# Gated DeltaNet layer on one core: the diagonal blocks of the chunk inverse reach V and T64 by VectorE block transposes with a strided output instead of through DRAM

## The chip, the cores and the metric

The kernel runs on one core of a Trainium2 chip. A core has five engines with instruction streams of their own: TensorE (PE; its weight loads are listed as PEld), VectorE (DVE), ScalarE (ACT), GpSimd (POOL) and SyncE (SP), which here only issues DMAs. Each engine works through its stream in order. The metric is the device time of one launch in microseconds (us).

## What is computed

The program has one layer (`DEPTH = 1`): RMSNorm, a gated DeltaNet mixer with its residual add, and a final RMSNorm, on 2048 tokens of width 1024, 8 heads of 128. The part that matters here is the chunked delta rule. In the reference a chunk has 64 tokens and the triangular matrix of each chunk and head is inverted by a solve:

```
a_mat = einsum("nbhid,nbhjd->nbhij", kb, k) * decay_strict
t_mat = triangular_solve(eye + a_mat, eye, left_side=True, lower=True, unit_diagonal=True)
u = t_mat @ (v * beta);   w = t_mat @ (kb * exp(g))
# then over the chunks of a head, one after the other:
v_new = u_c - w_c @ state
o_c   = qd_c @ state + attn_c @ v_new
state = state * gend_c + kend_c^T @ v_new
```

The kernel computes the same outputs with chunks of 128 tokens, so each inverse is 128 x 128.

## The kernel before, in words

**Tiling.** The sequence is cut into two super-blocks of 1024 tokens (`sb` 0 and 1). For each, `phase0` normalises and transposes x into `xh` and `xl` (a split of float32 into two parts that TensorE takes at full rate). Then come 16 units, one for each head and super-block: `project` (K, Q, V, Z; 24 matmuls of 128x512 for each of the eight outputs of a unit, and a short convolution behind K, Q and V), `decay` and `k_side` (the matrix U of each of the 8 chunks of the unit), `invert` (V, the inverse of 8 chunks), `v_side`, and `recur`, the serial loop over the 8 chunks: k S, then rho (DVE), then V rho, then n (ACT), then the update of S (DVE). `recur(u)` needs the V of its own unit; there are two V buffers, used in turn. At the end 16 output tiles (`out_tile`) are multiplied with w_out, 8 for each super-block; those of super-block 0 can run while the last units do.

**The inverse.** `invert` takes the four 32x32 diagonal blocks of each of the 8 chunks. They go through DRAM (`d1`) into the tile A, each block on four partitions; then 16 pairs of DVE instructions (TENSOR_TENSOR into a temporary, TENSOR_REDUCE into X) solve all blocks at once. Partition (i, c, g) of X holds rows 4m+g of block i of chunk c. The result has to go to two places: `T64` (blocks with the row on the partition, one buffer for all units) and the diagonal blocks of `V` (transposed). Then four groups of small matmuls build the off-diagonal parts: p1 (16 of 32x32, from T64), p2 (24 of 32x32, from V and Y), p3 (8 of 64x64, from T64), p4 (8 of 64x64, from V). ACT copies between them (Y, V), and one DVE copy writes the block of T64 that p3 needs.

**What sets the order.** All instructions are first recorded in a `Plan` with priorities, estimated durations and dependencies. `Plan.schedule` runs a list scheduler over them and `issue` emits them in the order found. So an edit in `invert` can move instructions everywhere. All instructions are emitted at one line, L354 of the profile; they are told apart by the tiles' names. In the profile `half` is the pool of 512-wide tiles (Y is one of them), `big` that of 1024-wide ones (A and U among them), `bank` a PSUM bank, `rnd` a split weight, `T` is T64, `d` is `d1` or `d2`. A float32 matmul shows as two records.

Of the kernel before, what the change touches and what calls it, by code (L numbers as in the profile page):

```python
# [29 lines left out]
C = SB // P  # L30
# [328 lines left out]
def tile_gated_deltanet(ctx: ExitStack, tc: tile.TileContext, x, a_norm_w, w_in, conv_w,  # L359
                        a_log, dt_bias, o_norm_w, w_out, final_w, consts, out):  # L360
    x, out, w_in, w_out = x[0], out[0], w_in[0], w_out[0]
# [12 lines left out]
    nc = Plan(tc, cp, pp, bufs, shared)  # L374
# [3 lines left out]
    def dram(tag, shape, bufs):  # L378
        n = turn.get(tag, 0)
        turn[tag] = n + 1  # L380
        if n < bufs:
            turn[tag, n] = dp.tile(shape, F32, name=f"{tag}{n}")
        return turn[tag, n % bufs]

    def st(shape, dtype, tag):
        return nc.tile(tag, shape, dtype)

    def ps(tag, shape=(P, TB)):
        a = nc.tile(tag, (P, TB), F32, psum=True)[0:shape[0], 0:int(np.prod(shape[1:]))]
        return a.rearrange("p (c k) -> p c k", k=shape[2]) if len(shape) > 2 else a  # L390
# [55 lines left out]
    T64 = cp.tile([P, C, 64], F32, name="T64")  # L446
# [196 lines left out]
    def chunked(a):  # L643
        return a.rearrange("p (c k) -> p c k", k=P)

    def bc(col, n=P):
        return col.unsqueeze(2).broadcast_to([P, col.shape[1], n])
# [73 lines left out]
    R = [slice(32 * i, 32 * i + 32) for i in range(4)]  # L721

    def invert(un):
        U, V = chunked(un["U"]), Vs[un["i"] % 2]

        d1 = dram("d1", [4, C, 32, 32], 2)
        for i in range(4):
            nc.sync.dma_start(d1[i].rearrange("c r k -> r c k"), U[R[i], :, R[i]])
        A = st([P, 32, 32], F32, "A")
        nc.sync.dma_start(A, d1.rearrange("i c r k -> (i c) (r k)").unsqueeze(1).broadcast_to([4 * C, 4, 1024]))  # L730

        nc.vector.memset(A.rearrange("p a b -> p (a b)")[:, ::33], 0.0)
        pair = st([P, 15, 32], F32, "pair")
        up = A.rearrange("p a b -> p (a b)")[:, 34:34 + 66 * 15:66]
        nc.vector.tensor_tensor(out=pair, in0=A[:, 2::2, :], in1=bc(up, 32), op=ALU.mult)
        nc.vector.tensor_tensor(out=A[:, 1:30:2, :], in0=A[:, 1:30:2, :], in1=pair, op=ALU.add)
        nc.vector.memset(A.rearrange("p a b -> p (a b)")[:, ::33], 1.0)
        X = st([P, 8, 32], F32, "X")
        nc.scalar.copy(X, rows4)
        for c in [*range(29, 0, -2), 0]:  # L740
            n, m0, w = 32 - c, c // 4, 2 if c else 1
            tmp = st([P, 8, 2, 32], F32, "pair")[:, m0:, 0:w, 0:n]
            nc.vector.tensor_tensor(out=tmp, in0=X[:, m0:, c:].unsqueeze(2).broadcast_to([P, 8 - m0, w, n]),
                                    in1=A[:, c:c + w, c:].unsqueeze(1).broadcast_to([P, 8 - m0, w, n]), op=ALU.mult)
            nc.vector.tensor_reduce(out=X[:, m0:, c:c + w], in_=tmp, axis=AX.X, op=ALU.add)
        d2 = dram("d2", [32, 4, C, 32], 2)
        for g in range(4):
            nc.sync.dma_start(d2[g::4].rearrange("m i c k -> (i c) m k"), X[g::4])
        for i in range(4):
            b = (i % 2) * 32  # L750
            nc.sync.dma_start(T64[R[i], :, b:b + 32], d2[:, i])
        for i in range(4):
            b = (i % 2) * 32
            nc.vector.transpose(out=V[R[i], :, R[i]], in_=T64[R[i], :, b:b + 32])
        p1 = ps("inv", (P, C, 32))
        nc.after = T64[R[2], :, 0:32],
        for c in range(C):
            nc.tensor.matmul(p1[R[1], c], lhsT=U[R[0], c, R[1]], rhs=T64[R[0], c, 0:32], start=True, stop=True)
            nc.tensor.matmul(p1[R[3], c], lhsT=U[R[2], c, R[3]], rhs=T64[R[2], c, 0:32], start=True, stop=True)
        Y = st([P, C, 64], F32, "Y")[:, :, 0:32]  # L760
        nc.scalar.copy(Y[R[1]], p1[R[1]])
        nc.scalar.copy(Y[R[3]], p1[R[3]])
        p2 = ps("inv", (P, C, 32))
        nc.after = Y[R[3]], V[R[3], :, R[3]]
        for c in range(C):
            nc.tensor.matmul(p2[R[0], c], lhsT=Y[R[1], c], rhs=V[R[1], c, R[1]], start=True, stop=True)
            nc.tensor.matmul(p2[R[2], c], lhsT=Y[R[3], c], rhs=V[R[3], c, R[3]], start=True, stop=True)
            nc.tensor.matmul(p2[R[1], c], lhsT=V[R[1], c, R[1]], rhs=Y[R[1], c], start=True, stop=True)
        nc.scalar.copy(V[R[0], :, R[1]], p2[R[0]])
        nc.scalar.copy(V[R[2], :, R[3]], p2[R[2]])  # L770
        nc.vector.tensor_copy(T64[R[1], :, 0:32], p2[R[1]])
        p3 = ps("inv", (P, C, 64))
        for c in range(C):
            nc.tensor.matmul(p3[64:128, c], lhsT=U[0:64, c, 64:128], rhs=T64[0:64, c], start=True, stop=True)
        Y2 = st([P, C, 64], F32, "Y")
        nc.scalar.copy(Y2[64:128], p3[64:128])
        p4 = ps("inv", (P, C, 64))
        for c in range(C):
            nc.tensor.matmul(p4[0:64, c], lhsT=Y2[64:128, c], rhs=V[64:128, c, 64:128], start=True, stop=True)
        nc.scalar.copy(V[0:64, :, 64:128], p4[0:64])  # L780
# [135 lines left out]
    for u in range(NU):  # L916
        un = dict(i=u, sb=u // H, h=u % H, xh=xhs, xl=xls, g=gt, w=w_first if u == 0 else {})
        last = u % H == H - 1
        nc.prio = float(u)
        if prev is not None:  # L920
            recur(prev)
        if u == 0:
            nc.prio = -0.72
        project(un, ((KI, 0), (QI, 0)), 2 if u == 0 else 1)
        nc.prio = float(u)
        decay(un)
        k_side(un, 0)
        project(un, ((KI, 1), (QI, 1)))
        k_side(un, 1)
        nc.prio = u - 0.5  # L930
        invert(un)
        nc.prio = float(u)
        project(un, ((VI, 0), (ZI, 0), (VI, 1), (ZI, 1)) if last else ((VI, 0), (VI, 1), (ZI, 0), (ZI, 1)))
        v_side(un)
        if last and u < NU - 1:
            nc.prio = u - 0.5
            xhs, xls, pba = phase0(u // H + 1)
            gt = gates(pba)
        prev = un
# [3 lines left out]
    for sb in range(NSB):  # L943
        for t in range(SB // P):
            i = sb * C + t
# [42 lines left out]
```

## Time and profile before

| | |
|---|---|
| median of 3 runs | 1285.72 us (1285.3 to 4319.13) |
| profiled execution, device time | 1284.4 us |
| its span, first to last instruction | 1282.6 us |
| mean granted clock of TensorE | 0.986 |
| busy: PE, PEld, DVE, ACT, POOL | 1245.6, 1041.1, 933.9, 615.1, 159.6 us |
| DMA: packets, of them under 512 B | 162439, 58817 |
| DMA: MB, share of 16 engines (q1) | 123.00, 32.7% |

Busy time is the time in which an engine has an instruction in work. The time outside the span is what the launch needs before its first and after its last instruction. TensorE has two clock levels, 1.2 and 2.4 GHz; a granted clock of 1.00 is the upper one, 0.50 the lower.

### The profile page before, as it was taken

The page shows a single profiled execution, that of the slowest core. Times are in us where ns is not written, and L with a number is a line of the kernel's source. Part 1 is how long each engine was busy: PE and PEld are TensorE (multiplying, and loading weights), DVE is VectorE, ACT ScalarE, POOL GpSimd, SP SyncE. Part 2 cuts the span into 40 slices and gives each one's busy share as a digit, 9 for nine tenths or more (in the row PEclk, how much of TensorE's full clock was granted, in tenths as well). Part 3 has the DMA queues.
Part 4 walks back from the last instruction along what each step waited for, and adds up shares of the span by engine and source line. Part 5 has one row for each costly group of instructions (what it writes and reads, how often), then busy time and mean ns, then how long its engine had stood idle before and what let it go on. Part 6 is the DMA issues. An engine that isn't in the chain of part 4 may idle for free.

```text
span 1282.6 us, 21318 instructions
## 1 busy us (share of the span) xinstructions
PE 1245.6 (97%) x8093; PEld 1041.1 (81%) x8093; DVE 933.9 (73%) x2181; ACT 615.1 (48%) x1301; POOL 159.6 (12%) x277
## 2 busy tenths in 40 slices
PE   6999799999999999989999999999999999999997
PEld 5788688888888888878887888888888888887886
DVE  5678677858776868786787787778777788854643
ACT  6664265544465436656543645453645464231221
POOL 4211011101011101120010101010101010101000
PEclk9999799999999999999998999999999999999999
DMA  7140432220433042422223323204222435545731
GB/s 221 34 113 22 103 82 76 67 78 18 120 81 124 14 122 77 119 51 85 79 52 90 86 63 74 72 14 120 76 83 52 167 94 172 183 156 173 255 106 66
DMA packets 162439, 123.00 MB, mean 96 GB/s; under 512 B 58817, under 2 KB 141346, under 8 KB 162338
## 3 DMA queue, kind: packets, MB, share of 16 engines
q1 hardware_dynamic: 162338, 121.66, 32.7%
q8 instruction: 63, 1.03, 0.3%
q14 instruction: 38, 0.31, 0.1%
HBM read 100.46 MB, written 21.17 MB: 95 GB/s over the span
## 4 chain that ended last, share of the span: by engine, by line
PE 93%; DVE 4%; ACT 1%; DMA 1%; issue 0%; SPq 0%; POOLq 0%; DVEq 0%; ACTq 0%
PE bank L354 93%; DVE half L354 2%; DVE X L354 1%; DVE big L354 1%; DMA big<-in_a_norm_w_dram 0%; DVE rnd L354 0%; DVE xl L354 0%; ACT half L354 0%; ACT rnd L354 0%; ACT xh L354 0%; SPq L354 0%; DMA d<-X 0%; DVE V L354 0%; ACT V L354 0%; ACT n L354 0%
## 5 line engine op out<-in xcount | busy, mean ns | idle before, releaser
L354 PE MATMUL bank<-xh,rnd 128*128 128x512 f32 (+1 forms) x2624 | 878.2, 404 | 6.1 <-ACT rnd L354 4.7
L354 PEld LDWEIGHTS bank<-xh,rnd 128*128 128x128 f32 x2624 | 484.8, 190 | 96.6 <-ACT rnd L354 5.3
L354 PE MATMUL bank<-xl,rnd 128*128 128x512 f32 (+1 forms) x1328 | 534.4, 403 | 0.8 <-DVE xl L354 0.8
L354 PEld LDWEIGHTS bank<-xl,rnd 128*128 128x128 f32 x1328 | 252.6, 190 | 46.0 <-DVE xl L354 1.6
L354 DVE SCALAR_TENSOR_TENSOR half<-raw,vcol,half 128x512 f32<-128x512 f32 x288 | 214.2, 746 | 64.5 <-ACT half L354 61.7
L354 ACT ACTIVATE half<-half 128x512 f32<-128x512 f32 x128 | 81.1, 633 | 94.2 <-DVE half L354 93.1
L354 ACT ACTIVATE n<-bank,nb 128x128 f32<-128x128 f32 x128 | 46.8, 366 | 145.1 <-PE bank L354 144.9
L354 ACT CAST rnd<-big 128x1024 fp32r<-128x1024 f32 x80 | 83.2, 1046 | 65.7 <-PE bank L354 46.0
L354 ACT COPY raw<-bank 128x512 f32<-128x512 f32 x96 | 56.4, 587 | 106.4 <-PE bank L354 105.9
L354 DVE TENSOR_TENSOR rnd<-big,rnd 128x1024 fp32r<-128x1024 f32 x80 | 97.4, 1218 | 12.9 <-ACT rnd L354 12.5
L354 DVE TENSOR_TENSOR half<-X,big 128x6 f32<-128x6 f32 (+15 forms) x256 | 94.8, 370 | 5.4 <-ACT X L354 1.4
L354 DVE TENSOR_REDUCE X<-half 128x2 f32<-128x6 f32 (+15 forms) x256 | 91.9, 359 | 4.1
L354 DVE SCALAR_TENSOR_TENSOR S<-S,dend,bank 128x128 f32<-128x128 f32 x128 | 44.0, 344 | 69.7 <-PE bank L354 69.0
L354 ACT ACTIVATE half<-big 128x512 bf16<-128x512 f32 (+1 forms) x48 | 37.1, 773 | 102.5 <-DVE big L354 56.7
L354 POOL COPY halo<-raw 128x3 f32<-128x3 f32 x72 | 21.7, 301 | 476.9 <-ACT raw L354 437.1
L354 ACT ACTIVATE half<-raw,vcol 128x512 f32<-128x512 f32 x96 | 69.3, 722 | 6.6 <-DVE vcol L354 1.5
L354 DVE SCALAR_TENSOR_TENSOR rho<-bank,eg,half 128x128 f32<-128x128 f32 x128 | 44.2, 345 | 31.2 <-PE bank L354 30.7
L354 PEld LDWEIGHTS bank<-n,half 128*128 128x128 f32 x256 | 47.2, 191 | 12.9 <-ACT n L354 3.3
L354 PEld LDWEIGHTS bank<-rho,V 128*128 128x128 f32 x256 | 47.5, 193 | 11.8 <-ACT V L354 1.7
L354 PEld LDWEIGHTS bank<-S,half 128*128 128x128 f32 x256 | 47.2, 193 | 11.7 <-DVE S L354 2.5
L354 POOL TENSOR_TENSOR sk<-ssk,phalf 128x4 f32<-128x4 f32 x32 | 35.4, 1107 | 157.3 <-DVE ssk L354 154.0
L354 ACT ACT_TABLE_LOAD x42 | 53.9, 1283 | 1.5 <-PEq L972 0.7
(113 smaller groups left out, 1558.1 us busy)
## 6 DMA issues: line engine op xcount, KB each, us to landing
big<-in_a_w_in_dram SPq DMA_DIRECT2D x64, 512.0 KB
big<-in_x_dram SPq DMA_DIRECT2D x32, 512.0 KB
big<-gd SPq DMA_DIRECT2D x16, 512.0 KB
half<-gd SPq DMA_DIRECT2D x32, 256.0 KB
big<-d SPq DMA_DIRECT2D x16, 512.0 KB
yd<-half SPq DMA_DIRECT2D x32, 256.0 KB
big<-yd SPq DMA_DIRECT2D x16, 512.0 KB
big<-rd SPq DMA_DIRECT2D x16, 512.0 KB
```

Of the source, the lines that this page charges most:

```text
L354: ins = getattr(getattr(self.tc.nc, op[6]), op[7])(*args, **kwargs)
```

## The change

The tile `d2` in DRAM goes, with its four DMAs from X and its four DMAs into T64 for each unit (128 in all). In their place DVE transposes X straight into the diagonal blocks of V: for block i the instruction reads 32 partitions (c, g) by 8 x 32 elements (m, k), transposes each 32x32 square, and writes partition k, so that element (m, c, g) lands at `V[k, c, 4m+g]`. The output is strided: runs of four float32, and after each run a jump to the next chunk. Then T64 is filled from V by three plain transposes (blocks 0, 2 and 1; the fourth block of T64 was read by nothing but the old transposes). Four DVE transposes from T64 to V go, seven come.

```diff
-        d2 = dram("d2", [32, 4, C, 32], 2)
-        for g in range(4):
-            nc.sync.dma_start(d2[g::4].rearrange("m i c k -> (i c) m k"), X[g::4])
         for i in range(4):
+            nc.vector.transpose(out=V[R[i], :, R[i]].rearrange("p c (m g) -> p m c g", g=4), in_=X[R[i]])
+        for i in (0, 2, 1):
             b = (i % 2) * 32
-            nc.sync.dma_start(T64[R[i], :, b:b + 32], d2[:, i])
-        for i in range(4):
-            b = (i % 2) * 32
-            nc.vector.transpose(out=V[R[i], :, R[i]], in_=T64[R[i], :, b:b + 32])
+            nc.vector.transpose(out=T64[R[i], :, b:b + 32], in_=V[R[i], :, R[i]])
```

The scheduler makes a new order of it on every engine. Up to the end of unit 0's X loop the order of PE and DVE is the old one; three later places are shown.

DVE, end of unit 0's X loop, before (X is reduced for the last time in the first row; `big_103` is A of unit 1; `half_454` a convolution):

```order
L354 TENSOR_REDUCE X_158<-half_647 128x8
L354 SCALAR_TENSOR_TENSOR half_454<-raw_115,vcol,half_454 128x512
L354 MEMSET big_103 128x32
L354 TENSOR_TENSOR half_482<-big_103 128x480
...
L354 STREAM_TRANSPOSE V_85<-T_84 32x8x32
L354 TENSOR_TENSOR half_647<-X_158,big_103 128x8x15
L354 TENSOR_REDUCE X_158<-half_647 128x4x2
L354 STREAM_TRANSPOSE V_85<-T_84 32x8x32
L354 TENSOR_TENSOR half_482<-X_158,big_103 128x10x17
```

and the same place now:

```order
L354 TENSOR_REDUCE X_156<-half_645 128x8
L354 SCALAR_TENSOR_TENSOR half_452<-raw_113,vcol,half_452 128x512
L354 STREAM_TRANSPOSE V_85<-X_156 32x8x8x4 x4
L354 STREAM_TRANSPOSE T_84<-V_85 32x8x32 x3
L354 MEMSET big_101 128x32
L354 TENSOR_TENSOR half_480<-big_101 128x480
```

The four old transposes stood between pairs of unit 1's X loop; the seven new ones stand in one piece ahead of that loop. In the other units they stand in one piece too.

PE, the inverse of unit 0 and the start of `recur(0)`, before (`bank_172<-xh,rnd` is the last of 24 projection matmuls into that bank):

```order
L354 MATMUL bank_172<-xh_337,rnd_491 128x512
L354 MATMUL bank_244<-T_84,big_142 32x32 x16
L354 MATMUL bank_238<-V_85,half_707 32x32 x2
...
L354 MATMUL bank_257<-T_84,big_142 64x64 x8
L354 MATMUL bank_167<-V_85,half_707 64x64 x8
L354 MATMUL bank_191<-rho_837,V_85 128x128
```

and now (of the 24 projections into that bank, now `bank_170`, nine stand ahead of p1; the others are in the gaps):

```order
L354 MATMUL bank_170<-xh_335,rnd_489 128x512
L354 MATMUL bank_242<-T_84,big_140 32x32 x16
L354 MATMUL bank_170<-xh_335,rnd_252 128x512
...
L354 MATMUL bank_236<-V_85,half_638 32x32 x2
...
L354 MATMUL bank_255<-T_84,big_140 64x64 x8
L354 MATMUL bank_170<-xh_335,rnd_489 128x512
L354 MATMUL bank_165<-V_85,half_705 64x64 x8
L354 MATMUL bank_189<-rho_835,V_85 128x128
```

Six projections now stand between p1 and p2, eight between p2 and p3, one between p3 and p4; before there was none. The p1 of unit 1 stands 24 matmuls behind the first rho of unit 0; before it stood 113 behind it.

DVE, the first output tile of super-block 1, before (`big_125<-big_125,big_112` applies the norm to it, `rnd_260` is its split; `big_119<-bank` is the residual add of the last tile of super-block 0, in two halves):

```order
L354 TENSOR_TENSOR big_119<-bank_201,big_119 128x512
L354 TENSOR_TENSOR big_119<-big_119,big_133 128x512
L354 TENSOR_SCALAR ss_150<-ss_150 128x1
L354 TENSOR_TENSOR big_119<-bank_191,big_119 128x512
L354 TENSOR_TENSOR big_125<-big_125,big_112 128x1024
...
L354 TENSOR_TENSOR rnd_260<-big_125,rnd_491 128x1024
```

and now (`big_131<-big_131,big_110`, `rnd_258`):

```order
L354 TENSOR_TENSOR big_140<-bank_242,big_140 128x512
L354 TENSOR_TENSOR big_131<-big_131,big_110 128x1024
...
L354 TENSOR_TENSOR rnd_258<-big_131,rnd_489 128x1024
L354 TENSOR_TENSOR big_101<-big_101,big_106 128x1024
L354 TENSOR_TENSOR big_140<-bank_165,big_140 128x512
```

Both now stand ahead of the second half's add instead of behind it. The last matmul of `recur` stands 22 matmuls earlier on PE than before, with as many projections more behind it.

## Rows read from the trace of the kernel before

**Rows 1.** The page, part 1: busy us (share of span) and instructions
```profile
PE 1245.6 (97%) x8093; PEld 1041.1 (81%) x8093; DVE 933.9 (73%) x2181; ACT 615.1 (48%) x1301; POOL 159.6 (12%) x277
```
**Rows 2.** The page, part 4: chain that ended last, by engine
```profile
PE 93%; DVE 4%; ACT 1%; DMA 1%; issue 0%; SPq 0%; POOLq 0%; DVEq 0%; ACTq 0%
```
**Rows 3.** Windows: stretch, length, busy us of each engine, PEclk, DMA share, GB/s
```profile
133.87:138.33 4.46, 1.11 (x39) 0.93 (x41) 4.13 (x13) 0.73 (x2) 0.00 (x0) 1.00 0.92 255
138.33:155.40 17.07, 12.99 (x103) 10.52 (x103) 10.12 (x20) 3.75 (x8) 0.00 (x0) 0.50 0.39 106
564.99:568.41 3.42, 3.32 (x8) 2.28 (x8) 3.35 (x7) 1.19 (x2) 1.56 (x1) 0.50 0.74 177
682.10:684.46 2.36, 1.24 (x7) 0.82 (x6) 2.06 (x7) 0.95 (x2) 0.00 (x0) 1.00 0.00 0
684.46:691.29 6.83, 5.59 (x19) 4.38 (x19) 6.52 (x16) 2.25 (x3) 0.00 (x0) 0.50 0.00 0
1186.22:1189.64 3.42, 3.42 (x10) 2.67 (x9) 2.25 (x3) 1.04 (x1) 0.00 (x0) 0.50 0.86 274
692.00:1181.00 489.00, 489.00 (x3298) 410.23 (x3297) 366.37 (x843) 226.09 (x489) 47.90 (x79) 1.00 0.35 103
1190.00:1275.00 85.00, 85.00 (x370) 68.92 (x368) 41.21 (x71) 16.82 (x36) 5.54 (x7) 1.00 0.42 143
```
**Rows 4.** Timeline of PE, unit 0: start, us, instruction, [idle before <- releaser]
```profile
133.87 0.84 PE L354 MATMUL bank<-T,big 32*32 32x32 f32 x32
...
135.82 0.22 PE L354 MATMUL bank<-V,half 32*32 32x32 f32 x2 [1.11 <-DVE V L354]
138.27 0.19 PE L354 MATMUL bank<-V,half 32*32 32x32 f32 x1 [2.23 <-DVE V L354]
...
141.05 1.97 PE L354 MATMUL bank<-T,big 64*64 64x64 f32 x16 [1.73 <-DVE T L354]
143.74 1.97 PE L354 MATMUL bank<-V,half 64*64 64x64 f32 x16 [0.72 <-ACT half L354]
146.38 0.80 PE L354 MATMUL bank<-rho,V 128*128 128x128 f32 x2 [0.67 <-ACT V L354]
```
**Rows 5.** Timeline of DVE, unit 0: end of the X loop, first old transpose
```profile
126.59 0.41 DVE L354 TENSOR_REDUCE X<-half 128x8 f32<-128x256 f32 x1
126.92 0.74 DVE L354 SCALAR_TENSOR_TENSOR half<-raw,vcol,half 128x512 f32<-128x512 f32 x1
...
134.31 0.42 DVE L354 STREAM_TRANSPOSE V<-T 32x256 f32<-32x256 f32 x1
```
**Rows 6.** Timeline of SP's queue: d2 of units 0 and 1
```profile
127.03 2.58 SPq L354 DMA_DIRECT2D d<-X  x4
131.08 1.79 SPq L354 DMA_DIRECT2D T<-d  x4
...
146.49 2.55 SPq L354 DMA_DIRECT2D d<-X  x4
```
**Rows 7.** Timeline of PE: first instruction behind the two later waits
```profile
563.47 1.10 PE L354 MATMUL bank<-ident,big 128*128 128x128 f32 x8 [3.11 <-POOL big L354]
...
1184.40 0.50 PE L354 MATMUL bank<-xh,rnd 128*128 128x512 f32 x1 [2.99 <-ACT rnd L354]
```
**Rows 8.** Timeline of DVE at the first output tile of super-block 1
```profile
1181.44 0.69 DVE L354 TENSOR_TENSOR big<-bank,big 128x512 f32<-128x512 f32 x1 [3.15 <-PE bank L354]
1182.05 1.82 DVE L354 TENSOR_TENSOR big<-big,big 128x1024 f32<-128x1024 f32 x2
```
**Rows 9.** Lines by form: count, busy us, mean ns, idle before
```profile
L354 DVE STREAM_TRANSPOSE V<-T 32x256 f32<-32x256 f32 x64 | 27.8, 434 | 1.5
L354 DVE TENSOR_TENSOR big<-big,nexpA 128x64 f32<-128x64 f32 x2 | 0.6, 276 | 0.1
L354 DVE TENSOR_TENSOR big<-big,dtb 128x64 f32<-128x64 f32 x2 | 0.4, 222 | 0.0
L354 ACT COPY half<-bank 32x256 f32<-32x256 f32 x32 | 11.7, 365 | 15.4 <-PE bank L354 11.5 <-DVE V L354 3.2
```

## The prediction

> **What bounds the kernel now.** I read the page first. TensorE is busy 1245.6 of 1282.6 us and VectorE 933.9 [rows 1], and the chain of waits that ended last is 93% TensorE [rows 2]. So time can only come from the 37.0 us in which TensorE has nothing, and from stretches at its lower clock. The windows by stage show where these are [rows 3]. From 692 to 1181 us TensorE is busy 489.00 of 489.00 us: inside the ordinary units no transfer and no VectorE instruction holds it up, whatever they take. The losses stand at four places:
>
> - the inverse of unit 0: idle 4.46 - 1.11 = 3.35 and 17.07 - 12.99 = 4.08, together 7.43 us; in the second window the granted clock is 0.50, the lower level, so the 12.99 us of work would take about half of that at the upper one: 6.5 us lost [rows 3].
> - the start of super-block 1: a wait of 3.11 us for POOL [rows 7], then 3.32 us of work at the lower level: 1.7 lost [rows 3].
> - a stretch from 682.10 to 691.29: idle 1.12 + 1.24 = 2.36, and 5.59 us at the lower level: 2.8 lost [rows 3].
> - the first output tile of super-block 1: a wait of 2.99 us [rows 7], and 3.42 us at the lower level: 1.7 lost [rows 3].
>
> That is 15.9 us of idle time and 12.7 us of clock, 28.6 in all. The other 21 us of idle time lie at the two ends (first loads, last tile), and the new order leaves the start as it is.
>
> The timeline of TensorE at unit 0 shows who is waited for [rows 4]. p1 starts at 133.87, straight behind a projection. Then p2 waits 1.11 and 2.23 us for DVE's writes of V, p3 waits 1.73 for DVE's copy into T64, p4 0.72 and rho 0.67 for ACT. DVE's timeline shows why the first two are long [rows 5]: X is done at 126.59 + 0.41 = 127.00, and the first of the four old transposes comes only at 134.31, with unit 1's loop around it. The two DMA steps lie between [rows 6].
>
> **Unit 0 until rho.** Of the 24 projections ahead of p1 nine are left there. A projection takes 85.00 us / 370 = 0.23 us [rows 3], so TensorE comes to p1 at 133.87 - 15 x 0.23 = 130.4. Is T64 ready by then? DVE finishes its convolution step at 126.92 + 0.74 = 127.66 [rows 5]; then come seven transposes. An old one of the same size lasts 434 ns [rows 9], and DVE instructions that don't need each other overlap by 0.08 us (the step starts 0.33 us behind the start of a reduce that lasts 0.41) [rows 5]. So seven take 7 x 0.355 = 2.5 us and end at about 130.2: p1 doesn't wait.
>
> The price of the strided output is not in the trace. The nearest rows are the old transpose, 434 ns, and a pair of TENSOR_TENSOR of 64 elements: the one with `nexpA` writes with a step of eight elements and takes 276 ns, the one with `dtb` writes densely and takes 222 [rows 9]: 54 ns, or 0.84 ns for each element with a step. If all 256 elements paid that, a strided transpose would take 0.22 us more and the seven 3.4 us; if only the 64 starts of runs paid, 0.05 more each and 2.7. Less than 2.5 is excluded, since no fewer elements are moved. I take 2.5, as three of four elements have their neighbour beside them; both ends stay in the range (p1 later by 0.7 at the far one).
>
> The Trainium skill ("SBUF — State Buffer", the note on cachelines in Door 1: The DMA port swizzle) says that accesses inside one 16-byte line go at full bandwidth and a move to a new line is penalised. The 54 ns of the row with a step agree; for runs of four float32, one line each, no run here shows it. By the rule at its best the seven stay at 2.5, by the row's price for each new line at 2.7.
>
> From p1 at 130.4: p1 0.84, p2 about 0.8, p3 and p4 half of 1.97 each [rows 4], so 3.6; 15 projections 3.45. Two ACT copies of 0.365 [rows 9] lie between p1 and p2 and again, with the DVE copy, between p2 and p3; six (1.4) and eight (1.8) projections cover them. Uncovered stay 0.72 - 0.23 = 0.5 before p4 and 0.67 before rho. Sum 8.2, rho at 138.6 instead of 146.38: **-7.8 us**.
>
> **Unit 0 from rho on.** Of the 4.08 us idle at the lower clock 3.12 lie before rho, so of the 9.02 us from rho to 155.40 about 8.06 are work, 4.0 lost. The order keeps ten serial matmuls of `recur` in a row here; the same row of ten at 682 cost 2.8 of clock. I take that again: **-1.2 us**.
>
> **Unit 1.** Its p1 now stands 24 matmuls behind rho, not 113. TensorE is there after the serial ten (about 6.5 us, by the stretch at 682) and 13 projections (3.0): at 148. Its X loop ended at 146.49 before, when SP could issue [rows 6], and four old transposes were in it; now seven follow it: 149.5. A new wait, **+1.5 us** (0 to 3).
>
> **The stretch at 682.** There ten serial matmuls stood in a row in the old order; in the new one unit 0 is the only such place. I take the whole **-5.2 us** (0 if the row of waits comes back elsewhere).
>
> **The first output tile of super-block 1.** DVE's multiply for it at 1182.05 stands behind an add that waits for TensorE's last matmul of the tile before [rows 8]. In the new order it stands ahead of that add, 24 projections or 5.5 us earlier for TensorE, and `recur` ends 22 matmuls (5.1 us) earlier, so its input is there too. 5.1 is over 2.99: **-4.7 us** with the clock (0 at worst).
>
> **The start of super-block 1.** POOL's multiply is released by nothing in the change. But p1 and p2 of unit 7 now stand there with nothing between, and two copies (0.73) bare. I take **0**, between -4.8 (gone) and +4 (one wait more of this kind).
>
> **The other units.** Three transposes more make 48 x 0.434 = 21 us of DVE, 75% of the span; SP loses 2.58 + 1.79 us of issuing per unit [rows 6] and 128 DMAs. TensorE covers both: it has no idle time there to win, and as long as each DVE step of `recur` comes in time, none to lose. **0**; what it costs without that cover is the second rival. Without the d2 wait in its queue SP issues weight loads earlier; TensorE waits for none now, so that brings nothing.
>
> **Sum.** -7.8 - 1.2 + 1.5 - 5.2 - 4.7 = -17.4: 1284.4 (the profiled execution) becomes 1267.0. The median is 1.3 higher, so I say **1268 us**, 1.4% less.
>
> **Rivals.**
>
> *The gain is given back* (0.20). Only unit 0 was caused by d2; the waits at 682 and 1184 are places where the list scheduler ran out of fill, and a new order can have others, as at the start of super-block 1. For it: every engine's order moved. Against: the new order shows only one such place. If two waits like those of rows 7 (4.8 with the clock) and that of 682 come back elsewhere, 14.8 of the 17.4 are gone: 1283.
>
> The Trainium skill ("Perfetto Trace Analysis", Identifying the Most-Contended Engine) says to work on the engine of highest occupancy, and to judge TensorE by its weight loads (81% here) and not by its matmuls. By it a change that takes from the DMAs and gives to DVE should bring nothing or cost: this rival. The 489 us without idle agree for the units; the waits at unit 0 don't.
>
> *The piece of seven holds up `recur`* (0.07). In the old order other work stood between the transposes; now S and rho steps behind the piece wait for all of it. A chunk's steps are covered by some 13 projections, 3.0 us; a piece of 2.5 fits, and at the far price of 3.4 each of 15 units loses 0.4, 6 us. Slower than before it gets when a unit loses 17.4 / 15 = 1.2 us, a piece of 4.2 us, or 0.78 us for a strided transpose. At 1.0 us each (2.1 lost per unit): 1300. Against it: 0.78 is beyond both ends of the rows, and DVE has 27% idle.
>
> *All four places vanish* (0.08): 1284.4 - 28.6 + 1.3 = 1257.
>
> **Numbers.** Forecast 0.65. The range is 1258 to 1285: the low end is nearly the floor, the high end takes in the first rival. A measurement of this kernel can tell about 2% from no change: under 1260.0 is faster, over 1311.4 slower. Faster 0.10 (the last rival and the edge of the forecast), slower 0.03 (the end of the second rival), same 0.87.
>
> **What would show it.** Right: p1 of unit 0 near 130.4 and rho near 139, no waits at 682 and before the first tile of super-block 1, a strided transpose near 0.43 us, 1.0 in the steady stretch. Wrong: TensorE waiting for DVE's S, rho or V in unit after unit, or a low clock at new places.

## The result and the profile after

The changed kernel takes 1269.95 us (median of 5 runs, 1267.44 to 1271.77), against 1285.72: ratio 0.9877, 95% interval 0.9861 to 0.9894. That is 15.8 us less: clear of no change by the interval, but under the 2% from which the forecast would have called it faster. The one run of the kernel before at 4319 us stands outside the ratio. The profiled execution is the slowest of the five: 1271.77 us, 12.6 under the profiled execution before, so the readings below explain 12.6 us and not 15.8.

The page, busy time of each engine and the DMA summary, of the changed kernel:

```profile
PE 1242.9 (98%) x8093; PEld 1039.9 (82%) x8093; DVE 954.2 (75%) x2229; ACT 615.5 (48%) x1301; POOL 173.0 (14%) x277
...
DMA packets 127623, 118.80 MB, mean 94 GB/s; under 512 B 24001, under 2 KB 106530, under 8 KB 127522
```

VectorE is 20.3 us busier than in [rows 1], as 48 transposes of 0.434 should make it; 34,816 small packets are gone. The chain that ended last is still TensorE's, by 96%. Where it lost time is in the windows of the changed kernel (stretch, length, busy us of PE, PEld, DVE, ACT, POOL, granted clock, DMA share, GB/s):

```profile
41.26:44.67 3.41, 3.41 (x8) 2.67 (x9) 3.38 (x6) 1.95 (x3) 0.74 (x2) 0.50 0.01 2
131.00:140.25 9.25, 8.35 (x131) 6.15 (x129) 8.13 (x28) 2.62 (x6) 0.00 (x0) 1.00 0.53 148
140.25:150.49 10.24, 8.02 (x27) 6.31 (x26) 9.61 (x21) 2.61 (x4) 0.00 (x0) 0.50 0.26 77
540.00:560.08 20.08, 16.48 (x167) 13.26 (x165) 19.37 (x41) 13.26 (x24) 8.13 (x7) 1.00 0.23 66
560.08:573.74 13.66, 13.66 (x66) 10.51 (x65) 4.77 (x8) 3.80 (x6) 2.08 (x1) 0.50 0.00 1
670.00:700.00 30.00, 30.00 (x170) 25.93 (x169) 21.83 (x57) 13.40 (x21) 0.41 (x2) 1.00 0.22 67
1170.00:1200.00 30.00, 30.00 (x132) 24.48 (x131) 21.73 (x33) 8.75 (x17) 1.65 (x3) 1.00 0.77 276
```

Length minus PE's busy time is idle; half of the busy time at 0.50 is lost to the clock. So unit 0 (131.00 to 150.49) costs 0.90 + 2.22 + 4.01 = 7.1 us, before 13.9 by [rows 3]. The stretches at 682 and at the first output tile are gone. The start of super-block 1 costs 3.60 + 6.83 = 10.4, before 5.0 (the 4.8 of [rows 3, 7] and small waits beside them). At 41.26 us a piece of lower clock has come up (1.7).

At the start of super-block 1 TensorE waits for several things in turn, at p1 and p2 of unit 7 first and then for the norm (its timeline in the changed kernel):

```profile
556.46 0.21 PE L354 MATMUL bank<-T,big 32*32 32x32 f32 x2 [1.20 <-ACT xh L354]
...
558.16 0.47 PE L354 MATMUL bank<-V,half 32*32 32x32 f32 x3 [0.59 <-DVE xl L354]
...
559.78 1.72 PE L354 MATMUL bank<-ident,big 128*128 128x128 f32 x8 [0.67 <-POOL big L354]
```

TensorE in unit 0, timeline of the changed kernel (answers to [rows 4]):

```profile
131.26 0.70 PE L354 MATMUL bank<-T,big 32*32 32x32 f32 x32
...
137.98 1.14 PE L354 MATMUL bank<-V,half 64*64 64x64 f32 x16 [0.23 <-ACT half L354]
139.79 0.49 PE L354 MATMUL bank<-rho,V 128*128 128x128 f32 x2 [0.67 <-ACT V L354]
...
143.08 0.80 PE L354 MATMUL bank<-S,half 128*128 128x128 f32 x2 [1.12 <-DVE S L354]
```

The waits for V and T64 are gone, those for ACT stand as forecast, and the update of S is a new one. VectorE's timeline there (answers to [rows 5]):

```profile
127.49 0.42 DVE L354 TENSOR_REDUCE X<-half 128x8 f32<-128x256 f32 x1
...
128.48 1.81 DVE L354 STREAM_TRANSPOSE V<-X 32x256 f32<-32x256 f32 x4
130.32 1.36 DVE L354 STREAM_TRANSPOSE T<-V 32x256 f32<-32x256 f32 x3
```

The seven take 3.2 us: from start to start 457 ns, 1.81 for four. The reduce above is 0.9 us later than before: at 40 us this execution was 0.7 us ahead (40.24 against 40.92 for the same matmul), and the lower clock that follows there costs 1.7.

### The profile page after: what moved, and what is told of

It reads as the page before. It is cut to its first block, busy times and chain, and to the rows that moved or that the text cites. A ratio compares the mean times of both kernels' runs of the same rounds, so it can differ in the third digit from the quotient of the medians.

```text
span 1270.0 us, 21157 instructions
## 1 busy us (share of the span) xinstructions
PE 1242.9 (98%) x8093; PEld 1039.9 (82%) x8093; DVE 954.2 (75%) x2229; ACT 615.5 (48%) x1301; POOL 173.0 (14%) x277
## 4 chain that ended last, share of the span: by engine, by line
PE 96%; DVE 2%; ACT 1%; DMA 0%; issue 0%; POOL 0%; SPq 0%; POOLq 0%; DVEq 0%; ACTq 0%
PE bank L354 96%; DVE half L354 1%; DMA big<-in_a_norm_w_dram 0%; DVE big L354 0%; ACT xh L354 0%; DVE xl L354 0%; ACT half L354 0%; POOL big L354 0%; DVE X L354 0%; ACT rnd L354 0%; DVE rnd L354 0%; ACT big L354 0%; SPq L354 0%; ACT n L354 0%; DVE sumo L354 0%
## 5 line engine op out<-in xcount | busy, mean ns | idle before, releaser
L354 POOL TENSOR_TENSOR sk<-ssk,phalf 128x4 f32<-128x4 f32 x32 | 39.5, 1233 | 123.2 <-DVE ssk L354 123.2
```

Source lines behind the costliest of these rows:

```text
L354: ins = getattr(getattr(self.tc.nc, op[6]), op[7])(*args, **kwargs)
```

## The experiments

Ratios are to the kernel before, each beside runs of it on the same chip. The theory that they tested: **the way through DRAM costs time only in units 0 and 8, the first of each super-block**, whose inverse cannot start before that super-block's norms and gates; every other inverse has started long before its V is wanted. The rivals: the waits at 682 and 1184 were accidents of the scheduler's order, or it is the DMA traffic that costs.

### Which units pay (three runs)

```diff
+        if un["i"] == 0:          # units 0 and 8: in (0, 8);  not unit 0: > 0
             (the seven transposes)
+        else:
+            (d2, its DMAs and the four old transposes)
```

> Unit 0 gets the transposes, units 1 to 15 keep the way through DRAM. Theory (first units): the way through DRAM costs time only where a unit's inverse cannot start early, which is at the first unit of each super-block, units 0 and 8; the stretch at 682 us of the kernel before is unit 8's. Then unit 0 gains its 6.6 to 7.8 us, the stretch at unit 8 stays (1.1 + 1.2 us of waits and 2.8 of clock), and the time is 1277 to 1279 us. Rival 1 (accident of the order): only unit 0 was caused by d2, the stretch at 682 is a place where the scheduler ran out of fill; then it has no reason to stay, and the time can be 1270 to 1279. Rival 2 (traffic): the gain comes from 35,000 DMA packets fewer in all units; then one unit of 16 gives 1 us: 1284 to 1285.

Measured: 1279.41 us, ratio 0.9946 (0.9929 to 0.9962).

> Units 0 and 8 (the first of each super-block) get the transposes, the other 14 keep the way through DRAM. Theory (first units): all of the gain that the change has by its cause, 6.6 to 7.8 at unit 0 and 5.2 at unit 8, is there with two units: 1270 to 1274 us, and no waits of S, rho or n in a row near 680 us. Rival 1 (accident of the order): as with unit 0 alone, 1270 to 1279, the stretch at 680 present or not. Rival 2 (traffic): two units of 16 give 2 us: 1283 to 1284.

Measured: 1273.17 us, ratio 0.9903 (0.9884 to 0.9922).

> Unit 0 keeps the way through DRAM, units 1 to 15 get the transposes. Theory (first units): unit 0's 6.6 to 7.8 us are lost again, the rest stays: 1276 to 1279 us, with 2 to 3.4 us of idle TensorE between the projections of unit 0 and its rho as before. Rival 2 (traffic): 15 of 16 units give the gain, 1270 to 1272.

Measured: 1276.50 us, ratio 0.9934 (0.9910 to 0.9957).

With unit 0 alone the row of serial matmuls is where it was. TensorE's timeline of that kernel, with the waits in brackets:

```profile
678.25 0.49 PE L354 MATMUL bank<-n,half 128*128 128x128 f32 x2 [0.46 <-ACT n L354]
...
680.23 0.49 PE L354 MATMUL bank<-rho,V 128*128 128x128 f32 x2 [0.34 <-DVE rho L354]
...
682.65 0.49 PE L354 MATMUL bank<-S,half 128*128 128x128 f32 x2 [0.76 <-DVE S L354]
```

With units 0 and 8 the same stretch has no gap (windows of that kernel):

```profile
674.00:688.00 14.00, 14.00 (x83) 12.12 (x82) 13.76 (x34) 4.07 (x7) 0.00 (x0) 1.00 0.26 77
```

And with unit 0 left out, its old wait is back (timeline of that kernel):

```profile
140.85 1.97 PE L354 MATMUL bank<-T,big 64*64 64x64 f32 x16 [1.71 <-DVE T L354]
```

Two of the three came out inside the theory's range, unit 0 alone 0.4 us above it. There unit 8's waits stayed as forecast (3.0 us idle), but without the 2.8 us of lower clock; between 1000 and 1200 us, where the kernel before loses 4.8, it loses 6.2. Two units of 16 give 12.8 of the 15.8 us, with 4,400 packets fewer instead of 34,800: traffic is out. What the other 14 units add lies within the intervals.

### The order shuffled, without the change and with it

```diff
-    HOP = ((0, 197, 230, ...), (456, 127, ...
+    HOP = ((0, 194, 227, ...), (456, 124, ...
```

The numbers are the planner's estimates, in ns, of the hop from one engine to the next; three of them go down by 3: TensorE to VectorE, TensorE to ScalarE, and VectorE to its own next instruction (the expectation of the second run names VectorE to TensorE; that one, 456, stays).

> The kernel before; in the planner alone the same hops are priced 3 ns lower. The way through DRAM stays in all units. Theory (first units): the waits of unit 0 and the row of serial matmuls in unit 8 near 682 us stay, since the two DMA steps make them; the wait ahead of the first output tile (1184 us) was an accident of the order and may go, and others may come (unit 14 has bare steps in this order): 1280 to 1288 us. Rival (accident of the order): the stretch at 682 goes as well, 1274 to 1281 us.

Measured on the kernel before: 1284.68 us, ratio 0.9993 (0.9981 to 1.0005). Its timeline and windows:

```profile
683.82 0.49 PE L354 MATMUL bank<-n,half 128*128 128x128 f32 x2 [0.46 <-ACT n L354]
...
688.19 0.49 PE L354 MATMUL bank<-S,half 128*128 128x128 f32 x2 [0.65 <-DVE S L354]
...
1067.45 1.14 PE L354 MATMUL bank<-T,big 64*64 64x64 f32 x16 [1.28 <-DVE T L354]
```

```profile
1068.48:1075.31 6.83, 6.16 (x29) 5.16 (x28) 2.02 (x2) 2.97 (x5) 0.00 (x0) 0.50 0.66 236
1170.00:1200.00 30.00, 30.00 (x132) 24.45 (x131) 19.30 (x29) 8.30 (x16) 1.95 (x2) 1.00 0.87 286
```

The waits at unit 8 stay (2.9 us idle, no lower clock), so they belong to the DRAM way. The wait before the output tile goes without the change, so its place was an accident of the order; but another takes its place near 1067, 2.8 us idle and 3.1 of clock. Between 1000 and 1200 us each of the four kernels whose last units go through DRAM loses 4.7 to 6.2 us (before 4.8, shuffled 5.9, unit 0 only 6.2, units 0 and 8 4.7), and of the eight with transposes there, each issued once, seven lose at most 0.7 and one, "not unit 7" below, 7.2. Whether the DRAM way of the last units makes these losses, or the orders do, no run tells apart.

> The changed kernel; in the planner alone the hop from TensorE to VectorE and ScalarE and from VectorE to TensorE is priced 3 ns lower, which shuffles the order. The transposes stay. In this order unit 0 reads as in the changed kernel, and p1 and p2 of unit 7 have some 1.4 us of projections between them, where the changed kernel has none. Theory (place): the changed kernel's loss at the start of super-block 1 (3.5 us of waits and 6.8 of clock) comes from that bare place, not from the transposes: it shrinks to 1 to 4 us in all, time 1262 to 1268 us; nothing comes back at 682 or 1184. Rival (lasting): the norms of super-block 1 stall TensorE whatever the order, 1268 to 1272 us.

Measured on the changed kernel: 1277.78 us, ratio 0.9939 (0.9920 to 0.9959). Here the theory on the place fails. p1 and p2 of unit 7 had projections between them, and TensorE waited longer than ever for the norms (timeline of that kernel; 0.67 in the changed one):

```profile
569.26 1.97 PE L354 MATMUL bank<-ident,big 128*128 128x128 f32 x8 [7.05 <-POOL big L354]
```

Three estimates 3 ns lower take back half of the gain.

### The start of super-block 1

```diff
# norms of super-block 1 earlier
-            nc.prio = u - 0.5
+            nc.prio = u - 0.6
# not unit 7: the seven transposes, else d2 and the four old ones
+        if un["i"] != 7:
# norms of super-block 1 on VectorE
-        if t % 2:
+        if t % 2 and i < 8:
```

> The changed kernel with one priority changed: the norms and gates of super-block 1 stand a tenth of a unit earlier than unit 7's inverse instead of level with it. The order of the units before and of unit 0 stays, and p1 and p2 of unit 7 get projections between them. Theory (place): the loss at the start of super-block 1 shrinks from 3.5 us of waits and 6.8 of clock to 1 to 4 us in all, 1262 to 1268 us. Rival (lasting): 1268 to 1272 us.

Measured: 1271.11 us, ratio 0.9883 (0.9863 to 0.9903). p1 and p2 don't wait, and the norm's wait grew from 0.67 to 3.71 us (timeline of that kernel): the waiting moved from one to the other. The bare place between p1 and p2 (no other matmul stood there) was not the cause; the rival's range has the time:

```profile
559.27 1.97 PE L354 MATMUL bank<-ident,big 128*128 128x128 f32 x8 [3.71 <-POOL big L354]
```

> The changed kernel, but unit 7 keeps the way through DRAM. Theory (cover at the start of super-block 1): with the transposes unit 7's p1 to p4 are done earlier, and are then missing as cover for TensorE while the norms of super-block 1 run; the loss there was 3.5 to 5.4 us in the orders in which unit 7 goes through DRAM and 7.6 to 11.8 where it does not. Here it goes back to 3.5 to 5.4 us in place of 10.3, all else stays: 1263 to 1266 us. Rival (norms alone): the loss depends on the chain of the norms and not on unit 7's way, it stays 7.6 to 11: 1268 to 1272 us.

Measured: 1267.80 us, ratio 0.9864 (0.9846 to 0.9882). 1.8 us above the theory's range and 0.2 below the rival's, so in neither. The loss at the place went, further than forecast (2.2 us idle, clock 1.00), and a new one came near 1090 us (windows of that kernel). The profiled execution is the slowest of its four, 1271.43 us with a mean clock of 0.989 against 0.993 and 0.994, so the other three may not have paid this new loss:

```profile
540.00:580.00 40.00, 37.78 (x306) 30.55 (x304) 32.15 (x76) 24.77 (x48) 14.46 (x12) 1.00 0.16 41
...
1092.61:1102.85 10.24, 10.24 (x48) 8.28 (x48) 4.97 (x7) 2.25 (x5) 1.47 (x1) 0.50 0.82 292
```

> The changed kernel, with every norm of super-block 1 multiplied on VectorE in one instruction (1.28 us); before, every second one goes over ScalarE (1.15) and POOL (2.35). Theory (norms alone): TensorE's waits at the start of super-block 1 are for POOL's multiply; the chain of an odd tile gets 2.2 us shorter and the waits of 3.5 us go down to 0 to 1.5, the lower clock behind them to half: 1262 to 1266 us. Rival (cover of unit 7): what is missing is TensorE's own work beside the norms, and VectorE gets 5 us more to do there: 1267 to 1272 us.

Measured: 1267.56 us, ratio 0.9870 (0.9853 to 0.9887). That is the rival's range. The wait for POOL is gone; 4.2 us of idle time and 3.4 us at the lower clock (1.7 lost) are left. TensorE now waits there at unit 7's p1, while VectorE does a norm, then the transposes, then the split `xl` that by the profile ended the wait; timelines of that kernel, TensorE, then VectorE:

```profile
558.56 0.69 PE L354 MATMUL bank<-T,big 32*32 32x32 f32 x32 [3.15 <-DVE xl L354]
```

```profile
552.49 1.28 DVE L354 SCALAR_TENSOR_TENSOR big<-big,rs,big 128x1024 f32<-128x1024 f32 x1
...
554.62 1.81 DVE L354 STREAM_TRANSPOSE V<-X 32x256 f32<-32x256 f32 x4
556.46 1.33 DVE L354 STREAM_TRANSPOSE T<-V 32x256 f32<-32x256 f32 x3
557.82 1.29 DVE L354 TENSOR_TENSOR xl<-bank,xh 128x512 fp32r<-128x512 f32 x2
```

> Both last edits together: unit 7 keeps the way through DRAM, and the norms of super-block 1 are multiplied on VectorE. Theory (the two losses at the start of super-block 1 are what the change gave back there): waits of 0 to 2 us and little or no low clock there, as with unit 7 alone, and no wait for POOL; if no new bare place comes up in this order, 1260 to 1265 us, under each of the two alone (1267.8, 1267.6). Rival (accident of the order): a place elsewhere, such as the 2.0 us of waits and 5.1 of clock that unit 14 paid when unit 7 alone was changed, takes it back: 1266 to 1270 us.

Measured: 1267.07 us, ratio 0.9852 (0.9835 to 0.9868); 2.1 us above the theory's range, in the rival's. The place itself does what the theory said (windows of that kernel):

```profile
0.00:60.00 60.00, 43.12 (x264) 38.15 (x265) 36.07 (x75) 37.85 (x65) 23.59 (x41) 0.97 0.45 136
540.00:580.00 40.00, 38.24 (x289) 29.41 (x287) 36.15 (x83) 23.82 (x45) 7.00 (x10) 1.00 0.16 40
```

What took it back is the first row: 16.9 us idle in the first 60, against 13.0 in the changed kernel, whose clock there is the same:

```profile
0.00:60.00 60.00, 46.98 (x272) 40.71 (x273) 35.50 (x79) 38.97 (x67) 23.76 (x41) 0.97 0.46 136
```

TensorE's first matmul waits for the first norm until 12.18 us, in the changed kernel until 9.04; why is open. The four executions of this kernel lie within 1.1 us of each other. The intervals of all three kernels overlap that of the changed one, so none of them is shown to beat it.

The loss between 495 and 592 us (idle plus half of the busy time at the lower clock), by what unit 7 does:

| unit 7 through DRAM | us | unit 7 by transposes | us |
|---|---|---|---|
| before | 5.0 | changed | 10.4 |
| before, shuffled | 3.8 | changed, shuffled | 15.5 |
| unit 0 only | 5.7 | not unit 0 | 8.1 |
| units 0 and 8 | 5.7 | norms earlier | 8.6 |
| not unit 7 | 2.2 | norms on VectorE | 5.9 |
| both edits | 2.3 | each element with a step (below) | 8.5 |

The columns don't overlap, but the twelve rows are not twelve orders: "unit 0 only" and "units 0 and 8" have the same order up to 654 us, and "not unit 0" and "each element with a step" keep the changed kernel's order there. So there are nine orders, and one order read 10.4, 8.1 and 8.5 in three executions, as the lower clock lasted 13.7 us in the first and 10.2 in the others. 5.7 and 5.9 nearly meet, the latter with the norms eased. The cleanest pairs differ in unit 7 alone and have one order up to its transposes at 554 us: 10.4 against 2.2, and 5.9 against 2.3. What in unit 7's transposes does it (their earlier p1 to p4, missing later as cover, or VectorE's time beside the norms) is not told apart; the wait above speaks for the second, in one order.

### How much cover the piece of seven has

```diff
-            ins = getattr(...)(*args, **kwargs)
+            for _ in range(2 if op[6] == "vector" and op[7] == "transpose" else 1):
+                ins = getattr(...)(*args, **kwargs)
```

> The changed kernel in its own order, with each VectorE transpose of the inverse issued twice: the piece of seven becomes one of 14, about 6.4 us of VectorE by the measured 457 ns from start to start, 3.2 more in each unit and 51 us more VectorE in all. Theory (TensorE covers it): only units 0 and 8, whose inverse is waited for, can pay, unit 0 about 3 us: 1270 to 1277 us. Rival (the piece holds up the recurrence): S and rho steps stand behind the piece in every unit, a chunk's steps are covered by some 3.0 us of projections, so each of 16 units loses up to 3.2: 1290 to 1320 us.

Measured: 1331.02 us, ratio 1.0353 (1.0324 to 1.0382). The theory that TensorE covers it is refuted. The rival's size was nearer, its place wrong: not S and rho wait but p1, in unit after unit. TensorE and VectorE of that kernel in one unit:

```profile
747.82 0.24 PE L355 MATMUL bank<-T,big 32*32 32x32 f32 x2 [1.24 <-DVE T L355]
748.76 0.69 PE L355 MATMUL bank<-T,big 32*32 32x32 f32 x30 [0.69 <-DVE T L355]
```

```profile
743.18 3.66 DVE L355 STREAM_TRANSPOSE V<-X 32x256 f32<-32x256 f32 x8
746.87 2.77 DVE L355 STREAM_TRANSPOSE T<-V 32x256 f32<-32x256 f32 x6
```

Next, the same with the planner told the price:

```diff
-                return n / 0.96 + 85, 0.0, False
+                return 2 * (n / 0.96 + 190), 0.0, False
```

> The kernel with each transpose twice, and the planner told so: it prices a transpose at 2 x 457 ns instead of 352. Same instructions as the kernel with each twice, another order. Theory (place in the order): TensorE has the work to cover 6.4 us of transposes in a unit, and the 1331 us came from p1 standing 1.2 us too early behind a piece that the planner took for 2.5 us; told the truth it puts other matmuls ahead of p1: no wait of 1.3 + 0.7 us at p1 in unit after unit, 1275 to 1295 us (unit 0 pays 3, units 5 and 14 have bare steps in this order). Rival (no cover): VectorE is the bound inside the units once it has 3.2 us more, 1320 to 1335 us.

Measured: 1300.96 us, ratio 1.0119 (1.0101 to 1.0137): 6 us above the theory's range and 20 under the rival's. From 880 to 1060 us the work is covered where it is planned, and not where it isn't (windows of the two kernels, planned first):

```profile
880.00:1060.00 180.00, 180.00 (x1151) 150.67 (x1150) 141.37 (x340) 90.98 (x199) 19.88 (x35) 1.00 0.27 81
```

```profile
880.00:1060.00 180.00, 173.93 (x1217) 146.01 (x1217) 137.80 (x324) 86.94 (x188) 18.65 (x29) 0.98 0.27 78
```

So TensorE had the cover; the fixed order had not put it there. What stays of the loss stands at new bare places, the largest at unit 14's p1, a wait of 5.38 us.

### The price of the strided output

```diff
-out=V[R[i], :, R[i]].rearrange("p c (m g) -> p m c g", g=4), in_=X[R[i]]
+out=V[R[i], :, R[i]].rearrange("p c (m g) -> p m g c", g=4), in_=X[R[i]].rearrange("p m (g c) -> p m g c", g=4)
```

> The changed kernel in its own order; the four transposes out of X write the two inner dimensions of the output the other way round, so that each element lies 512 bytes from the one before it (in the change, runs of four lie together). The same places of V are filled, with values in the wrong order. Theory (a step has a price): the row of the kernel before with a step of eight elements gives 0.84 ns for each such element, 256 of them 0.22 us: 650 ns for a transpose instead of 434, 0.86 us more per unit, inside the 1.2 us that p1 has behind the piece: 1270 to 1272 us. Rival (a step costs nothing): 434 ns, 1270 us. If an element costs twice that, 870 ns: the piece is 1.8 us longer and p1 waits 0.6 us with its clock in unit after unit: 1280 to 1290 us.

Measured: 1276.85 us, ratio 0.9943 (0.9927 to 0.9959). Lines by form (count, busy us, mean ns, idle before) of the changed kernel, then of this one:

```profile
L354 DVE STREAM_TRANSPOSE V<-X 32x256 f32<-32x256 f32 x64 | 27.8, 434 | 1.3
L354 DVE STREAM_TRANSPOSE T<-V 32x256 f32<-32x256 f32 x48 | 20.8, 434 | 1.5
```

```profile
L354 DVE STREAM_TRANSPOSE V<-X 32x256 f32<-32x256 f32 x64 | 40.2, 629 | 1.3
```

Runs of four cost nothing against [rows 9], a jump at every element 195 ns, 0.76 for each. The sizes were forecast well (0.84), the time was not: 0.78 us more per unit should have fitted in before p1, and it cost some 7 us by the medians. TensorE around p1 and VectorE's piece, of the changed kernel, then of this one:

```profile
779.82 0.40 PE L354 MATMUL bank<-xh,rnd 128*128 128x512 f32 x1
780.14 0.69 PE L354 MATMUL bank<-T,big 32*32 32x32 f32 x32
```

```profile
776.80 1.81 DVE L354 STREAM_TRANSPOSE V<-X 32x256 f32<-32x256 f32 x4
778.64 1.37 DVE L354 STREAM_TRANSPOSE T<-V 32x256 f32<-32x256 f32 x3
```

```profile
782.35 0.40 PE L354 MATMUL bank<-xh,rnd 128*128 128x512 f32 x1
782.68 0.91 PE L354 MATMUL bank<-T,big 32*32 32x32 f32 x32
```

```profile
779.33 2.59 DVE L354 STREAM_TRANSPOSE V<-X 32x256 f32<-32x256 f32 x4
781.95 1.37 DVE L354 STREAM_TRANSPOSE T<-V 32x256 f32<-32x256 f32 x3
```

p1 needs the first two of the three T64 pieces. In the changed kernel the second ends at 778.64 + 0.457 + 0.434 = 779.53, 0.6 us ahead of p1; with a step at 782.84, 0.16 behind p1's start, and p1 takes 0.91 us instead of 0.69. The margin is some 0.6 us in this unit and its neighbours, not the 1.2 that the expectation took from p1's two waits in the run with each twice (3.2 - 1.24 - 0.69). By the same sum it is 0.4 to 1.2 us in twelve units of the changed kernel, under 0.2 in units 0 and 2, and in units 7 and 8 p1 starts before its second block is there; unit 8's takes 0.94 us in place of 0.69 (TensorE's timeline of the changed kernel):

```profile
653.46 0.94 PE L354 MATMUL bank<-T,big 32*32 32x32 f32 x32
```

And none of these rows shows idle time, since the matmuls' modelled ends overlap: a stretch that reads busy throughout can still hold small waits. The step run reads 499.49 us busy of 500 (window of that kernel), with p1 late in unit after unit:

```profile
680.00:1180.00 500.00, 499.49 (x3329) 417.77 (x3329) 390.09 (x898) 229.01 (x493) 54.72 (x79) 1.00 0.32 99
```

## Why the prediction was right

The forecast was 1268 us; 1269.95 came, inside the range. The range of 1258 to 1285 holds the first rival as well, so the time alone does not show that the reasons were right; the terms do. Each in the two profiled executions:

| term | predicted us | measured us |
|---|---|---|
| unit 0 until rho | -7.8 | rho -6.6; -7.5 if counted from the end of X, which came 0.9 later |
| unit 0 after rho, with unit 1 | -1.2 + 1.5 | all of unit 0 and unit 1: -6.8 |
| stretch at 682 | -5.2 | -5.2 |
| first output tile | -4.7 | -4.7 |
| start of super-block 1 | 0 | +5.4 |
| lower clock at 41 us | not seen | +1.7 |

- **Unit 0 until rho** held, with one size wrong: the seven were taken at 0.355 us from start to start and took 0.457, since transposes don't overlap one another as the reduce and the convolution did [rows 5]. p1 did not wait, by luck: its second block of T64 was there at 130.32 + 0.457 + 0.434 = 131.21, 0.05 us ahead of it.
- **After rho** the lower clock again cost 4.0 us, not the 2.8 taken from the stretch at 682, and recur's S waited 1.12 us behind unit 1's X loop on VectorE. The expected wait of unit 1's p1 (+1.5) did not come. The terms together give -6.8, forecast -7.5.
- **The stretch at 682** was right in size and half wrong in reason. The text held it, as a place where the scheduler ran out of fill, for something that a new order may or may not have. It was unit 8's wait for d2: the waits, 2.4 us before, stay in the shuffled kernel before (2.9) and with unit 0 alone (3.0), and go with units 0 and 8. The 2.8 us of clock behind them came in the first of the three alone.
- **The first output tile** was as forecast in size. That its place was an accident is right, as shuffling the kernel before removes the wait. Whether the gain is one too is open: a loss of 4.7 to 6.2 us stays near the end in each of the four kernels whose last units go through DRAM.
- **The start of super-block 1** is the term that was mis-sized: 0, with bounds of -4.8 and +4, and it cost 5.4 in this execution, outside them; in the two kernels that keep this order there it cost 3.1 and 3.4, inside. The text saw the bare p1 and p2 of unit 7 and took them as the risk. They did wait (1.20, 0.20 and 0.59 us), but in the two runs that gave them cover the wait for the norm grew instead; taking the change out of unit 7 helped (2.2 us).
- **The other units** at 0: right at 434 ns, by a margin of 0.4 to 1.2 us in most units. That nothing holds TensorE up there, "whatever they take", was read from 489.00 us busy of 489.00 and was too strong: the step run and the run with each twice refute it. The second rival put the cover at 3.0 us, ahead of S and rho; the runs showed p1 as the one that waits. A piece of 3.2 us costs nothing that shows as idle time, one of 4.0 (the step run) some 7 us.
- **The gain is given back** happened in part: 5.4 at super-block 1, for the reason named, another order, but at a place that the transposes of unit 7 make. So one of the signs of being wrong came too, a lower clock at new places (41 and 560 us).

The table's terms sum to about -9.6, against a forecast of -17.4; the profiled executions differ by 12.6. Over the whole span idle time falls from 37.0 to 27.1 us (1270.0 - 1242.9) and the loss to the lower clock from 12.7 to 12.5, some 10.0 in all. The other 2.6 us stand nowhere as idle time or low clock. The step run shows that waits of this size can hide under modelled ends; that these do is not shown. That the median came within 2 us of the forecast is in part luck: 7.1 us of new losses that the sum did not have were offset in part by these 2.6 and by a median 1.8 under the profiled execution.

On the rule of one 16-byte line ("SBUF — State Buffer" in the Trainium skill, the note on cachelines): the trace agrees, 434 ns for runs of four float32, one line each, as for dense rows, and 629 when each element lands on a new line. On judging TensorE by its weight loads and not by its matmuls ("Perfetto Trace Analysis" in the Trainium skill, Identifying the Most-Contended Engine): the step run agrees that matmul busy time hides losses, with 499.49 of 500 us busy. From its other half, that the engine of highest occupancy is the one to work on, the prediction drew that the change should bring nothing. That does not follow: TensorE is that engine, by its weight loads too (81% against VectorE's 73% [rows 1]), and what the change shortened was a wait of that engine in two places; it brought 1.2%.

## What to carry to other kernels

Ask of each latency in which iterations it can be started early; it costs only where nothing can be put ahead of it, and here that was 2 units of 16. With a static order, "covered" means covered up to where the consumer was placed: look for the margin between the producer's end and the consumer's start (0.6 us here in unit after unit), not for the idle share of the engine. And when an edit goes through a list scheduler, shuffle the order of the old and the new kernel alike before crediting the edit with what moved: 3 ns in three estimates were worth 0.6% in the new kernel and nothing in the old.

## What the runs showed of the hardware

- A 32x256 float32 block transpose takes 434 ns, dense or with runs of four, and 629 ns with a jump of 512 bytes at each element; those of 434 follow each other at 457 ns from start to start.
- The granted clock did not follow from the order alone. The five executions of the changed kernel have mean clocks from 0.988 to 0.992. Behind the same two gaps of TensorE at 38 to 41 us (0.32 and 0.96 us) it fell to 0.50 for 3.41 us in the changed kernel's profile and stayed at 1.00 in the profile of units 0 and 8. Row after row of waits at unit 8 brought 6.83 us of lower clock before [rows 3] and none in the shuffled kernel before.
